# Two rings of weight buffers at fixed remainders, and another order of summing a pair's chunks

## The chip, the cores and the metric

The kernel runs on one core of one Trainium2 chip. The metric is the device time of the whole kernel in microseconds (us), as the median of several runs. Names used below: PE is TensorE, DVE is VectorE, ACT is ScalarE, SP the engine that issues the DMAs of the weights.

## The reference

Two layers work on x of 256 tokens by 1024 channels, all in float32. Each layer is a mixer and a ConvFFN, each followed by a layer norm. Cut to what matters here:

```python
def mixer_sublayer(x, ...):
    proj = x @ w_in        # RG-LRU input and GeLU gate, q/kv latents, rotary key, gates A and B
    y_rnn = jax.nn.gelu(g_rnn) * rg_lru(causal_dwconv(x_rnn, conv_w, conv_b), gx_w, gx_b, ...)
    y_mla = mla_attention(q_lat, kv_lat, k_rope, cos, sin, ...)
    merged = jax.nn.sigmoid(gate_a) * y_rnn + jax.nn.sigmoid(gate_b) * y_mla
    return merged @ w_out

def conv_ffn(x, w_up, ffn_conv_w, ffn_conv_b, w_down):
    h = causal_dwconv(x @ w_up, ffn_conv_w, ffn_conv_b)     # 1024 -> 6144
    h_gate, h_val = jnp.split(h, 2, axis=-1)
    return (jax.nn.gelu(h_gate) * h_val) @ w_down           # 3072 -> 1024

x = layer_norm(ALPHA * x + mixer_sublayer(x, ...), ...)
x = layer_norm(ALPHA * x + conv_ffn(x, ...), ...)
```

## The kernel before

Every float32 number is held as a sum of two numbers of the type fp32r, hi and lo, and a product is made of three matmuls: hi by hi, hi by lo and lo by hi (`mm3`, L193 to L196). Activations are kept as xhi and xlo, which begin at multiples of 256 bytes.

Weights come as raw tiles of 128 by 2048 numbers. SP loads one by `load_raw` (L156) into one of four raw buffers. `load_split` then splits it, half block by half block (1024 columns): ACT copies the raw half to hi (L185), DVE subtracts hi from raw to get lo (L186). A half block's hi and lo lie side by side in one tile `w` (L180), in a ring of six buffers. Each buffer is 8320 bytes long, so that the six begin, in the built program, at the remainders 192, 64, 192, 64, 192, 64 modulo 256. A half block takes the next buffer of the ring. Most raw tiles have two halves; a few have one, and after these the next raw tile's first half lies in the other sort of buffer. In layer 0's FFN, of 18 pairs that directly follow a down projection, six have their blocks at (192, 64), five at (64, 64) and seven at (192, 192); in layer 1's, twelve lie at (192, 64) and six at (64, 192).

A pair (`proj_pair`, L516 to L531) is one raw tile's product: 256 output channels, in two halves m of 128, by 1024 input channels in eight chunks kc. The first half block holds chunks 0 to 3, the second 4 to 7, each for both halves m. The loop at L525 runs over kc in order, so the 48 matmuls of a group (each of 256 columns) take 12 from the first block, 12 from the second, and the same again for the other m. The mixer's input projections call it (`g`, `x`, `ga`, `gb` in the ORDER table) and so does the up projection of the FFN, `up(j)` (L888); there a group is followed by 12 matmuls of 512 columns of the down projection (`dacc`). The weights of the down projection are split in the same way into other tiles (`wsh`, `wsl`). Other users of the `w` ring are the latent, q, k, v and output weights.

The order of PE is the written one. ACT, DVE and SP follow an order that a scheduler sets when the program is built, from its own estimates; a tile's reuse, and so the remainders, are set there too. Each engine works off its list in order and waits where an operand or a buffer isn't ready. In the mixer's recurrence, the convolved input is split into xch by ACT (L610) and xcl by DVE (L611), the block-diagonal gates multiply them on PE (`gates`), and L629 and L631 make the sigmoid gate sg and its product gl.

Of the kernel before, what the change touches and what calls it, by code (L numbers as in the profile page):

```python
# [11 lines left out]
F32 = mybir.dt.float32  # L12
F32R = mybir.dt.float32r
# [4 lines left out]
P = 128  # L18
# [3 lines left out]
KC = D // P  # L22
# [27 lines left out]
HELD = 4  # L50
WARM = 8
LINE = 256
STEP = 32
KORD = (0, 1, 4, 5, 2, 3, 6, 7)
NPAIR = DFF // P
ALPHA = (2 * DEPTH) ** 0.25
# [69 lines left out]
def trunk(ctx, tc, x_tok, x_chan, pos, wts, par, lnrow, consts, out):  # L126
# [8 lines left out]
    wpool = ctx.enter_context(tc.tile_pool(name="wpool", bufs=1))  # L135
# [4 lines left out]
    def slot(name, dt=F32):  # L140
        return big.tile([P, 1024], dt, tag="t4", name=name, bufs=19, align_bytes=LINE)

    def bank(name):
        return pp.tile([P, 512], F32, tag="pb", name=name)
# [4 lines left out]
    def load_raw(l, key, parts=None, between=None):  # L149
        o, n = WOFF[key]  # L150
        raw = wpool.tile([P, 2048], F32, tag="raw", name=f"raw{l}", bufs=4, align_bytes=LINE)
        src = wts[l, o:o + P * n].rearrange("(p n) -> p n", p=P)
        for i, (a, b) in enumerate(parts or ((0, n),)):
            if between and b == n:
                between()
            nc.sync.dma_start(out=raw[:, a:b], in_=src[:, a:b])  # L156
        return raw
# [3 lines left out]
    def behind(ins, first):  # L161
        if first is not None:
            tc.add_manual_dep(ins.ins, first.ins.name, no_sync, reason="issue order")

    last_split = [None]
    ready = [(None, None)]
    later = [False]

    def load_split(l, key, cuts, in_slots=False, after=(None, None),
                   step=1024, parts=None, between=None):  # L170
        raw = load_raw(l, key, parts, between)
        if later[0]:
            after = ready[0]
        n = WOFF[key][1]
        res = []
        for a, b in cuts:
            if in_slots:
                hi, lo = slot("wsh", F32R), slot("wsl", F32R)
            else:
                both = wpool.tile([P, 2048 + STEP], F32R, tag="w", name="w", bufs=6)  # L180
                hi, lo = both[:, :1024], both[:, 1024:2048]
            for c in range(a, b, step):
                d = min(c + step, b)
                h, w = hi[:, c - a:d - a], raw[:, c:d]
                behind(A.activation(h, w, AF.Copy), after[0])  # L185
                lo_ins = V.tensor_tensor(out=lo[:, c - a:d - a], in0=w, in1=h.bitcast(F32),  # L186
                                         op=ALU.subtract)
                behind(lo_ins, after[1])
                last_split[0] = lo_ins
            res.append((hi, lo))  # L190
        return res

    def mm3(o, lh, ll, rh, rl, start, stop):  # L193
        T.matmul(o, lhsT=lh, rhs=rh, start=start, stop=False)  # L194
        T.matmul(o, lhsT=lh, rhs=rl, start=False, stop=False)  # L195
        T.matmul(o, lhsT=ll, rhs=rh, start=False, stop=stop)  # L196
# [19 lines left out]
    def latent_weights(l, i, **kw):  # L216
        r = load_split(l, ("lat", i), ((0, LATW), (LATW, 2 * LATW)), l > 0 and i == 3, **kw)
        return [(2 * i + j, r[j]) for j in range(2)]
# [128 lines left out]
    def xsl(xs, kc, a=0, b=S):  # L347
        hi, lo = xs[kc // 4]
        o = (kc % 4) * S
        return hi[:, o + a:o + b], lo[:, o + a:o + b]  # L350
# [160 lines left out]
    for l in range(DEPTH):  # L511
# [3 lines left out]
        def fetch(key):  # L515
            held[key] = load_split(l, key, ((0, 1024), (1024, 2048)), after=ends)  # L516

        def proj_pair(key, r=None):
            if r is None:
                if key not in held:  # L520
                    fetch(key)
                r = held.pop(key)
            ps = bank("proj")
            for m in range(2):
                for kc in range(KC):  # L525
                    hi, lo = r[kc // 4]
                    o = (kc % 4) * 256 + m * P
                    rh, rl = xsl(xs, kc)
                    mm3(ps[:, m * S:(m + 1) * S], hi[:, o:o + P], lo[:, o:o + P],
                        rh, rl, kc == 0, kc == KC - 1)  # L530
            return ps  # L531

        gl = [slot("gl") for _ in range(2)]
# [1 line left out]
        def gelu_branch(i):  # L535
            ps = proj_pair(("g", i))
            act_step(A.activation(gl[i // 2][:, (i % 2) * 512:(i % 2) * 512 + 512], ps,
                                  AF.Gelu_apprx_tanh))
# [56 lines left out]
        def conv_branch(i):  # L595
            ps = proj_pair(("x", i))
            for m in range(2):
                c = 2 * i + m
                dst = xc[c // 4][:, (c % 4) * S:(c % 4) * S + S]
                src = ps[:, m * S:(m + 1) * S]  # L600
                A.activation(dst, src, AF.Identity, scale=pcol(l, "cw", 24 + c),
                             bias=pcol(l, "cb", c))
                for k in range(1, 4):
                    conv_end.append(V.scalar_tensor_tensor(
                        out=dst[:, k:], in0=src[:, :S - k], scalar=pcol(l, "cw", 8 * (3 - k) + c),
                        in1=dst[:, k:], op0=ALU.mult, op1=ALU.add,
                    ))
                xh = sm.tile([P, S], F32R, tag="k1", name="xch", bufs=13, align_bytes=LINE)
                xl = sm.tile([P, S], F32R, tag="k1", name="xcl", bufs=13, align_bytes=LINE)
                A.activation(xh, dst, AF.Copy)  # L610
                V.tensor_tensor(out=xl, in0=dst, in1=xh.bitcast(F32), op=ALU.subtract)  # L611
                xsp[c] = (xh, xl)
# [13 lines left out]
        def gate_branch(i):  # L626
            ps = proj_pair(("ga", i))
            sg = slot("sg")[:, :512]
            act_step(A.activation(sg, ps, AF.Sigmoid))  # L629
            dst = gl[i // 2][:, (i % 2) * 512:(i % 2) * 512 + 512]  # L630
            V.tensor_tensor(out=dst, in0=dst, in1=sg, op=ALU.mult)  # L631
# [52 lines left out]
        def group_begin(g):  # L684
            r = load_split(l, ("qk", g), ((0, GRP_A), (GRP_A, GRP_N)),
                           after=(None, turned[0]))
            q96 = slot("q96")[:QK].rearrange("p (h s) -> p h s", h=4)
            k96 = slot("k96")[:QK].rearrange("p (h s) -> p h s", h=4)
            nc.sync.dma_start(out=k96[NOPE:], in_=krot[:, None, :].to_broadcast([ROPE, 4, S]))
            qk[g] = (r, q96, k96)  # L690
# [373 lines left out]
```

## Time and profile before

| | |
|---|---|
| runs | 785.43, 785.65, 787.75 us; median 785.65 |
| profiled execution | 786.62 us, its span 784.8 us |
| PE busy | 770.5 us (98%) |
| DVE busy | 646.0 us (82%) |
| ACT busy | 510.2 us (65%) |
| chain that ended last | PE 89%, DVE 4%, ACT 4% |
| proj matmuls | 3648 of 256 columns, 278 ns each as recorded |

A matmul's record is longer than the distance from one start to the next, since matmuls are pipelined: the pace is read from the starts in the timeline. "Idle" before an instruction stands in brackets with the engine and operation that ended it. PEclk is the granted clock of PE, 1.00 being 2.4 GHz and 0.50 being 1.2 GHz.

### The profile page before, as it was taken

How to read it: one execution, taken by the hardware profiler on the slowest of the kernel's cores; microseconds unless marked ns; L12 is line 12 of the kernel's file. 1: busy time of each engine (PE TensorE's matmuls, PEld its weight loads, DVE VectorE, ACT ScalarE, POOL GpSimd, SP SyncE). 2: the span in 40 equal slices, each digit the busy share in tenths (PEclk: the TensorE clock that was granted, in tenths of full speed). 3: DMA queues.
4: the chain of work that ended last, by engine and by line, in shares of the span. 5: the costliest groups of instructions: out<-in, count | busy, mean ns of one | idle time of the engine just before them, and what ended most of it. 6: DMA issues, size and time to landing. Idle time of an engine off the chain costs nothing.

```text
span 784.8 us, 14452 instructions
## 1 busy us (share of the span) xinstructions
PE 770.5 (98%) x5712; PEld 723.9 (92%) x5712; DVE 646.0 (82%) x1260; ACT 510.2 (65%) x910; POOL 10.2 (1%) x27
## 2 busy tenths in 40 slices
PE   9999899999999999999999999999999999999996
PEld 9999899878999999999899999998799999999994
DVE  6998789997699977668777897999877998677665
ACT  6856887783677565556374579688657775565540
POOL 0000000000000000000000000000000000000000
PEclk9999999999999999999999999999999999999999
DMA  9855436525457555535715554463515675746311
GB/s 320 331 210 215 151 112 240 207 63 210 162 199 262 203 199 210 195 126 196 268 52 218 169 208 134 172 231 123 193 76 186 261 251 182 247 162 200 123 54 54
DMA packets 26467, 144.76 MB, mean 184 GB/s; under 512 B 3360, under 2 KB 7072, under 8 KB 11808
## 3 DMA queue, kind: packets, MB, share of 16 engines
q1 hardware_dynamic: 26400, 143.84, 51.7%
q8 instruction: 45, 0.74, 0.4%
q14 instruction: 22, 0.18, 0.1%
HBM read 140.68 MB, written 1.05 MB: 181 GB/s over the span
## 4 chain that ended last, share of the span: by engine, by line
PE 89%; DVE 4%; ACT 4%; issue 2%; DMA 1%; SPq 0%; DVEq 0%
PE proj L196 16%; PE proj L194 15%; PE proj L195 15%; PE dacc L194 6%; PE dacc L195 6%; PE dacc L196 6%; PE oacc L194 2%; PE oacc L196 2%; PE oacc L195 2%; PE sps L759 2%; DVE w L186 2%; PE yps L802 2%; PE ptp L787 1%; PE latp L195 1%; PE latp L196 1%
## 5 line engine op out<-in xcount | busy, mean ns | idle before, releaser
L196 PE MATMUL proj<-xhi,w 128*128 128x256 f32 x1216 | 338.0, 278 | 3.0 <-DVE w L186 3.0
L194 PE MATMUL proj<-xhi,w 128*128 128x256 f32 x1216 | 338.1, 278 | 0.0
L195 PE MATMUL proj<-xlo,w 128*128 128x256 f32 x1216 | 337.7, 278 | 0.0
L186 DVE TENSOR_TENSOR w<-raw,w 128x1024 fp32r<-128x1024 f32 (+5 forms) x226 | 241.8, 1087 | 52.4 <-ACT w L185 51.9
L185 ACT ACTIVATE w<-raw 128x1024 fp32r<-128x1024 f32 (+5 forms) x226 | 208.8, 952 | 86.6 <-PE proj L196 73.4
L196 PEld LDWEIGHTS proj<-xhi,w 128*128 128x128 f32 x1216 | 228.8, 188 | 3.4 <-DVE w L186 3.4
L195 PEld LDWEIGHTS proj<-xlo,w 128*128 128x128 f32 x1216 | 229.2, 189 | 1.3
L194 PEld LDWEIGHTS proj<-xhi,w 128*128 128x128 f32 x1216 | 228.9, 188 | 1.4
L905 DVE SCALAR_TENSOR_TENSOR u<-proj,par,u 128x255 f32<-128x255 f32 (+1 forms) x176 | 83.4, 478 | 25.4 <-ACT u L902 23.3
L902 ACT ACTIVATE u<-proj,par 128x256 f32<-128x256 f32 x88 | 49.7, 564 | 72.7 <-DVE u L905 47.8
L194 PE MATMUL dacc<-wsh,hh 128*128 128x512 f32 x192 | 75.2, 392 | 0.0
L195 PE MATMUL dacc<-wsl,hh 128*128 128x512 f32 x192 | 75.1, 391 | 0.0
L196 PE MATMUL dacc<-wsh,hl 128*128 128x512 f32 x192 | 74.7, 389 | 0.0
L186 DVE TENSOR_TENSOR wsl<-raw,wsh 128x1024 fp32r<-128x1024 f32 (+2 forms) x66 | 70.4, 1077 | 0.0
L185 ACT ACTIVATE wsh<-raw 128x1024 fp32r<-128x1024 f32 (+2 forms) x66 | 59.5, 938 | 0.0
L196 PEld LDWEIGHTS dacc<-wsh,hl 128*128 128x128 f32 x192 | 36.1, 188 | 7.8
L194 PEld LDWEIGHTS dacc<-wsh,hh 128*128 128x128 f32 x192 | 36.0, 188 | 6.4
L195 PEld LDWEIGHTS dacc<-wsl,hh 128*128 128x128 f32 x192 | 36.1, 188 | 6.0
L199 ACT ACTIVATE hh<-u 128x256 fp32r<-128x256 f32 x48 | 19.8, 411 | 24.7 <-DVE u L913 24.6
L194 PE MATMUL oacc<-w,mhi 128*128 128x512 f32 x64 | 26.7, 417 | 0.0
L196 PE MATMUL oacc<-w,mlo 128*128 128x512 f32 x64 | 25.3, 395 | 0.0
L195 PE MATMUL oacc<-w,mhi 128*128 128x512 f32 x64 | 25.2, 393 | 0.0
(213 smaller groups left out, 1130.2 us busy)
## 6 DMA issues: line engine op xcount, KB each, us to landing
raw<-in_wts SPq DMA_DIRECT2D x114, 1024.0 KB, 4.9
raw<-in_wts SPq DMA_DIRECT2D x8, 832.0 KB, 4.9
gb<-in_lnrow SPq DMA_DIRECT2D x8, 512.0 KB, 7.7
raw<-in_wts SPq DMA_DIRECT2D x4, 672.0 KB, 4.0
raw<-in_wts SPq DMA_DIRECT2D x7, 336.0 KB, 6.1
raw<-in_wts SPq DMA_DIRECT2D x4, 512.0 KB, 4.8
xres<-in_x_tok SPq DMA_DIRECT2D x2, 512.0 KB, 6.0
k<-krot SPq DMA_DIRECT2D x8, 128.0 KB, 2.4
```

The lines of the kernel that those rows point to most:

```text
L185: behind(A.activation(h, w, AF.Copy), after[0])
L186: lo_ins = V.tensor_tensor(out=lo[:, c - a:d - a], in0=w, in1=h.bitcast(F32), op=ALU.subtract)
L194: T.matmul(o, lhsT=lh, rhs=rh, start=start, stop=False)
L195: T.matmul(o, lhsT=lh, rhs=rl, start=False, stop=False)
L196: T.matmul(o, lhsT=ll, rhs=rh, start=False, stop=stop)
L199: A.activation(hi, src, AF.Copy)
L759: T.matmul(sps[:, P:P + S], lhsT=q96[:, h4, P:], rhs=k96[:, h4], start=True, stop=True)
L787: T.transpose(ptp[:, b * P:(b + 1) * P], sns[hh][:, b * P:(b + 1) * P], ident)
L802: T.matmul(yps[hh * 64:hh * 64 + 64, t * P:S], lhsT=vs[:, hv:hv + 64], rhs=pts[hh][:, 2 * t * P:(2 + t) * P], start=t == 0, stop=t == 1)
L902: ea = A.activation(dst, src, AF.Identity, scale=pcol(l, "fw", 96 + ch), bias=pcol(l, "fb", ch))
L905: ev = V.scalar_tensor_tensor(out=dst[:, k:], in0=src[:, :S - k], scalar=pcol(l, "fw", 48 * (2 - k) + ch), in1=dst[:, k:], op0=ALU.mult, o ...
```

## The change

The ring of six `w` buffers becomes two rings of three: `w0` for the first half block of a raw tile, `w1` for the second. The buffers are 8192 bytes long, and a tile of 128 bytes stands between the two rings. In the built program the `w0` buffers all begin at 192 modulo 256, the `w1` buffers all at 64; the activations still begin at multiples of 256. A pair sums its chunks in the order 0, 4, 5, 1, 2, 3, 6, 7, for both m.

```diff
@@ -50,7 +50,8 @@
 LINE = 256
-STEP = 32
+GAP = 32
+PORD = (0, 4, 5, 1, 2, 3, 6, 7)
 KORD = (0, 1, 4, 5, 2, 3, 6, 7)
@@ -162,6 +163,7 @@
+    gap = []
     last_split = [None]
@@ -173,11 +175,13 @@
-        for a, b in cuts:
+        for i, (a, b) in enumerate(cuts):
             if in_slots:
                 hi, lo = slot("wsh", F32R), slot("wsl", F32R)
             else:
-                both = wpool.tile([P, 2048 + STEP], F32R, tag="w", name="w", bufs=6)
+                if i and not gap:
+                    gap.append(wpool.tile([P, GAP], F32, name="gap"))
+                both = wpool.tile([P, 2048], F32R, tag=f"w{i % 2}", name=f"w{i % 2}", bufs=3)
                 hi, lo = both[:, :1024], both[:, 1024:2048]
@@ -522,12 +526,12 @@
             for m in range(2):
-                for kc in range(KC):
+                for kc in PORD:
                     hi, lo = r[kc // 4]
                     o = (kc % 4) * 256 + m * P
                     rh, rl = xsl(xs, kc)
                     mm3(ps[:, m * S:(m + 1) * S], hi[:, o:o + P], lo[:, o:o + P],
-                        rh, rl, kc == 0, kc == KC - 1)
+                        rh, rl, kc == PORD[0], kc == PORD[-1])
```

Lines behind the edit stand four later in the new kernel: L186 is L190 there, L525 is L529.

On PE, a group of layer 0's FFN begins so before; `w_3748` is its first half block, `w_3751` its second:

```order
L194 MATMUL proj_3754<-xhi_2359,w_3748 128x256
L195 MATMUL proj_3754<-xlo_2360,w_3748 128x256
L196 MATMUL proj_3754<-xhi_2359,w_3748 128x256
...
L194 MATMUL proj_3754<-xhi_2361,w_3751 128x256
L195 MATMUL proj_3754<-xlo_2362,w_3751 128x256
L196 MATMUL proj_3754<-xhi_2361,w_3751 128x256
```

and so in the new kernel, where `w0_3749` and `w1_3752` are the same two half blocks:

```order
L198 MATMUL proj_3755<-xhi_2360,w0_3749 128x256
L199 MATMUL proj_3755<-xlo_2361,w0_3749 128x256
L200 MATMUL proj_3755<-xhi_2360,w0_3749 128x256
L198 MATMUL proj_3755<-xhi_2362,w1_3752 128x256
L199 MATMUL proj_3755<-xlo_2363,w1_3752 128x256
L200 MATMUL proj_3755<-xhi_2362,w1_3752 128x256
```

The first three rows stand four times before the second block's first; now they stand once.

On ACT, at layer 1's gates, the order before is this; `raw1_5548` is the weight tile whose halves are `w_5550` and `w_5553`, `gates_5573` a gate bank:

```order
L622 ACTIVATE ga_4875<-gates_5573,par1_168 128x256
L185 ACTIVATE w_5550<-raw1_5548 128x1024
L610 ACTIVATE xch_5458<-xc_4872 128x256
L185 ACTIVATE w_5553<-raw1_5548 128x1024
L629 ACTIVATE sg_5631<-proj_5582 128x512
L622 ACTIVATE gx_4874<-gates_5634,par1_168 128x256
```

and this in the new kernel:

```order
L626 ACTIVATE ga_4876<-gates_5574,par1_169 128x256
L189 ACTIVATE w0_5551<-raw1_5549 128x1024
L189 ACTIVATE w1_5554<-raw1_5549 128x1024
L633 ACTIVATE sg_5632<-proj_5583 128x512
L614 ACTIVATE xch_5459<-xc_4873 128x256
L626 ACTIVATE gx_4875<-gates_5635,par1_169 128x256
```

The copy to xch has moved behind the second half block and sg; on DVE xcl has likewise moved behind both lo halves and the product gl.

On DVE, ahead of layer 1's last gate pair, the order before is this; `raw1_6009` is that pair's weight tile, `w_6011` its first half block and `w_6014` its second:

```order
L186 TENSOR_TENSOR w_5971<-raw1_5969,w_5971 128x768
L664 SCALAR_TENSOR_TENSOR th_5742<-ga_4876,gx_4874 128x1024
L186 TENSOR_TENSOR w_5974<-raw1_5969,w_5974 128x896
L186 TENSOR_TENSOR w_5982<-raw1_5980,w_5982 128x1024
L186 TENSOR_TENSOR w_6011<-raw1_6009,w_6011 128x1024
L186 TENSOR_TENSOR w_6014<-raw1_6009,w_6014 128x1024
```

and this in the new kernel:

```order
L190 TENSOR_TENSOR w0_5972<-raw1_5970,w0_5972 128x768
L668 SCALAR_TENSOR_TENSOR th_5743<-ga_4877,gx_4875 128x1024
L190 TENSOR_TENSOR w1_5975<-raw1_5970,w1_5975 128x896
L190 TENSOR_TENSOR w0_5983<-raw1_5981,w0_5983 128x1024
L190 TENSOR_TENSOR w1_6015<-raw1_6010,w1_6015 128x1024
L190 TENSOR_TENSOR w0_6012<-raw1_6010,w0_6012 128x1024
```

The two halves of that pair have changed places, the second block's being split first; layer 0's last gate pair has the same exchange.

## Rows read from the trace of the kernel before

**Rows 1.** The page, part 1: busy us of each engine (share), xinstructions
```profile
PE 770.5 (98%) x5712; PEld 723.9 (92%) x5712; DVE 646.0 (82%) x1260; ACT 510.2 (65%) x910; POOL 10.2 (1%) x27
```

**Rows 2.** Two FFN windows: us, busy PE PEld DVE ACT POOL, PEclk, DMA, GB/s
```profile
229.60:377.00 147.40, 147.40 (x1069) 139.11 (x1068) 119.26 (x185) 91.03 (x137) 0.00 (x0) 1.00 0.59 206
614.50:763.00 148.50, 148.50 (x1081) 139.71 (x1080) 116.87 (x181) 87.13 (x133) 0.00 (x0) 1.00 0.53 187
```

**Rows 3.** DVE and PE, layer 1's last gate pair: start us, us, instruction
```profile
498.66 5.34 DVE L186 TENSOR_TENSOR w<-raw,w 128x896 fp32r<-128x896 f32 x5
...
502.05 0.38 PE L196 MATMUL proj<-xhi,w 128*128 128x256 f32 x1 [1.51 <-DVE w L186]
```

**Rows 4.** Timeline of PE, ends of four groups (columns as in Rows 3)
```profile
55.10 0.28 PE L194 MATMUL proj<-xhi,w 128*128 128x256 f32 x1
...
60.54 0.28 PE L194 MATMUL proj<-xhi,w 128*128 128x256 f32 x1
...
246.36 0.28 PE L194 MATMUL proj<-xhi,w 128*128 128x256 f32 x1
...
252.01 0.40 PE L194 MATMUL dacc<-wsh,hh 128*128 128x512 f32 x1
...
254.74 0.28 PE L194 MATMUL proj<-xhi,w 128*128 128x256 f32 x1
...
256.51 0.28 PE L194 MATMUL proj<-xhi,w 128*128 128x256 f32 x1
...
260.25 0.40 PE L194 MATMUL dacc<-wsh,hh 128*128 128x512 f32 x1
...
622.84 0.28 PE L194 MATMUL proj<-xhi,w 128*128 128x256 f32 x1
...
628.38 0.40 PE L194 MATMUL dacc<-wsh,hh 128*128 128x512 f32 x1
```

**Rows 5.** DVE and PE, one split of layer 0's FFN and its group
```profile
287.09 1.22 DVE L186 TENSOR_TENSOR w<-raw,w 128x1024 fp32r<-128x1024 f32 x1
...
304.81 0.28 PE L194 MATMUL proj<-xhi,w 128*128 128x256 f32 x1
```

**Rows 6.** Timeline of ScalarE (ACT), VectorE and PE at layer 1's gates
```profile
468.05 1.06 ACT L185 ACTIVATE w<-raw 128x1024 fp32r<-128x1024 f32 x1 [2.09 <-PE proj L196]
469.01 0.40 ACT L610 ACTIVATE xch<-xc 128x256 fp32r<-128x256 f32 x1
...
469.15 1.23 DVE L186 TENSOR_TENSOR w<-raw,w 128x1024 fp32r<-128x1024 f32 x1 [0.67 <-ACT w L185]
470.29 0.42 DVE L611 TENSOR_TENSOR xcl<-xc,xch 128x256 fp32r<-128x256 f32 x1
470.62 1.22 DVE L186 TENSOR_TENSOR w<-raw,w 128x1024 fp32r<-128x1024 f32 x1
471.76 0.68 DVE L631 TENSOR_TENSOR gl<-gl,sg 128x512 f32<-128x512 f32 x1
472.36 0.61 DVE L640 TENSOR_SCALAR ga<-ga,kl 128x256 f32<-128x256 f32 x2
...
471.36 0.28 PE L195 MATMUL gates<-xcl,w 128*128 128x256 f32 x1
```

**Rows 7.** Timeline of VectorE and PE, first pair of layer 0, then its gates
```profile
20.79 1.22 DVE L186 TENSOR_TENSOR w<-raw,w 128x1024 fp32r<-128x1024 f32 x1
...
21.63 0.28 PE L196 MATMUL proj<-xhi,w 128*128 128x256 f32 x1
...
84.59 0.58 PE L195 MATMUL gates<-xcl,w 128*128 128x256 f32 x1 [1.44 <-DVE xcl L611]
```

**Rows 8.** Windows, around waits of layer 0 (columns as in Rows 2)
```profile
80.94:84.53 3.59, 1.52 (x9) 0.92 (x7) 3.59 (x8) 3.59 (x8) 0.00 (x0) 1.00 0.83 281
84.53:87.94 3.41, 3.35 (x15) 3.35 (x16) 3.16 (x7) 3.41 (x7) 0.00 (x0) 0.50 0.38 104
115.10:118.50 3.40, 1.89 (x16) 1.69 (x16) 3.40 (x4) 0.73 (x2) 0.00 (x0) 1.00 0.86 289
```

## The prediction

> **What bounds the kernel now.** I read first the busy times of the page [rows 1], then the two long stretches of the ConvFFN by windows [rows 2], then TensorE's instructions one by one. TensorE is busy for 770.5 of 784.8 us; in the two FFN windows it is busy for the whole of 147.40 and 148.50 us, while VectorE has 119.26 and 116.87 and ScalarE 91.03 and 87.13. In these stretches only TensorE's own pace counts, and a nanosecond a matmul is felt in full. In the two mixers it waits now and then for a half block that ScalarE and VectorE have yet to split; 1.51 us for a VectorE split is the kind [rows 3].
>
> That pace differs between groups of the same 48 matmuls [rows 4], the reader's first thing to see. A group is a pair's 48 matmuls of 256 columns; its length is the start of what follows less its own start. One inside the mixer takes 60.54 − 55.10 = 5.44, or 113.3 ns a matmul. In the FFN the one at 246.36 takes 5.65 (117.7 ns), the one at 254.74 5.51, the one at 622.84 5.54. What differs is where the two weight buffers lie. With (192, 192) all 48 run at 117.7, and so do the five (64, 64) groups. With (192, 64) the first 15, up to 256.51, take 1.77 or 118 ns each, and the other 33 take 3.74 or 113.3: the pace turns three matmuls after the step from the 192 block to the 64 block, and it stays fast when the group goes back to 192 for the second half. With (64, 192) the step from 192 to 64 comes only after 24 matmuls, and the gain is smaller. Of 30 such steps in slow stretches I found 29 with this turn; a step from 64 to 192 never made it. A mixer group that directly follows a fast one is fast throughout, whatever its blocks. Why the memory does this no row says; I use it as a pattern.
>
> **The change, part by part.** No matmul, copy or load is added; there are as many on each engine as before.
>
> *Pace.* Every pair now is (192, 64), and the step from 192 to 64 comes after 3 matmuls, so a group that starts slow should have some 6 slow matmuls and 42 fast ones: 5.44 + 6 × 0.0045 = 5.47. Layer 0's FFN: seven (192, 192) and five (64, 64) groups, 12 × 0.18 = 2.1; six (192, 64), 6 × 0.04 = 0.2. Layer 1's: twelve (192, 64), 0.5, and six (64, 192), 6 × 0.075 = 0.45. Outside the FFN, the slow (64, 64) group at layer 1's start is as long as the one at 246.36 and saves 0.18, the three behind it, the last pair of layer 0's mixer and the first FFN pair of either layer about 0.85 together (from nothing for a group fast already to 0.2). In all 4.3, between 1.2 (the pace turns only at the second step from 192 to 64, after 18 matmuls) and 5.6 (all of them wholly fast). In the FFN nothing is late next: a lo half that VectorE splits at 287.09 is first used by the group at 304.81 [rows 5], so that needing the second block 1.0 us earlier and letting the first go 0.7 us later stay covered. SP's loads wait for raw buffers, which those splits free, with the same cover.
>
> *Waits.* The second block is wanted after 3 matmuls, not 12: 9 × 0.1133 = 1.0 us earlier. The first is let go at position 6 of 8 of the second half, not at 4: 6 × 0.1133 = 0.7 us later. ScalarE takes its work in a fixed order, and each wait on a buffer holds what stands behind it.
> (a) The last pair of a mixer's gate branch waits 1.51 for its first block, in a run of five VectorE splits of 5.34 [rows 3]. The order now has the second block of that pair split ahead of the first, so the lo half that TensorE wants comes one split later: 5.34/5 = 1.07, and 1.14 for a full half; +1.1 in each layer. In layer 0 this wait is set by VectorE's queue, so that lesser delays of TensorE ahead of it (below) are swallowed by it.
> (b) Layer 1's gates. ScalarE now copies w0, w1 and does sg before xch. From [rows 6]: w0 starts at 468.05 + 0.68 (its buffer is free later); two copies at 0.96 (469.01 less 468.05) and sg at about 0.5 put xch near 471.2, ahead of VectorE's turn. VectorE then has w0, w1 and the gated product ahead of xcl: 469.15 + 0.68 + 1.14 + 1.14 (471.76 less 470.62) + 0.60 (472.36 less 471.76) = 472.7, and 0.42 for xcl itself makes 473.1. TensorE wants xcl at 471.36 and waits for nothing now. It will wait 1.75. Behind it the next pairs queue, and ScalarE and VectorE wait for those, so most of the loss goes on; I add 0.2 for a second block that then comes just late.
> (c) The first pair: the lo half of its second block starts at 20.79 on VectorE and is done by 22.0; the sixth matmul, now the first to want it, stands at 21.63 [rows 7]. +0.4. (d) Layer 0's gates: xcl stands behind two splits and more; today TensorE waits 1.44 there. From nothing (rope work is put earlier) to 2.4 (two splits at 1.2); I take 0.2. (c) and (d) go into the wait (a).
> Sum: 1.1 + 1.75 + 0.2 + 1.1 = 4.15, say 4.3 with what of (c) and (d) isn't swallowed; from 2.3 (two times 1.1) to 6.7.
>
> *Clock.* After a stretch of 3.59 us with 1.52 busy the granted clock stood at 0.50, the 1.2 GHz level, for 3.41 us, with 16 weight loads, 213 ns a matmul in place of 113: 16 × 0.1 = 1.6. After the 1.51 wait (1.89 busy of 3.40) it stayed at 1.00 [rows 8]. With 1.1 more of waiting the same 3.40 has about 0.8 busy, nearer to the first. There are two such places and a new wait at the gates. Below nothing, above three times 1.6 = 4.8; I take one, 1.6, since the stretch that fell had several waits in a row.
>
> Sum: −4.3 + 4.3 + 1.6 = +1.6. The profiled execution took 786.62, 0.97 above the median 785.65 of its runs; on it 788.2, on the median 787.2.
>
> **The rivals.** *No half-speed stretch*: the same sum without the 1.6, 785.6. For it: the two waits of 1.51 caused none. *Two*: 788.8; for it: both long waits are alike, so one seldom falls alone.
> *The pace turns late* (the slower side). Its place is every group of the FFN: three matmuls on the 192 block may be too few to bring the turn, which no row shows with fewer than 12; then the second step, after 18 matmuls, brings it, and a group takes 5.44 + 21 × 0.0045 = 5.54. The 12 slow groups gain 0.11 each, 1.3; the 18 of (192, 64) lose 0.03 each, 0.5; the six (64, 192) stand still; some 0.4 elsewhere: 1.2 in place of 4.3, and 785.65 − 1.2 + 4.3 + 1.6 = 790.3. It decides from a group length of about 5.51 on, today's. Against it: the turn comes with the first 64 block each time, three matmuls in.
> *The waits of layer 1 are paid once* (faster). If VectorE loses little by TensorE's 1.75 at the gates, then the wait of (a) shrinks by it, as in layer 0, and layer 1 costs 1.2 in place of 3.0: 785.65 − 4.3 + 2.4 = 783.7 without a half-speed stretch, and 783.0 with groups that are fast from their first matmul on (30 × 0.025). For it: VectorE's splits run back to back there; against: ScalarE's work in between waits for TensorE's groups.
> *Placement decides nothing*: what differs is which block follows which operation, the buffers' remainders merely go with it, and the gain is 0: 785.65 + 4.3 + 1.6 = 791.5. The Trainium skill, "SBUF — State Buffer", section "SBUF: two separate sides", speaks for this one: TensorE, ScalarE and VectorE's dedicated pair never wait on one another. By that rule 5.65 and 5.51 for the same group should not differ; the trace has them [rows 4], so the rule, as far as I can apply it, disagrees with the measurement here.
>
> **How the numbers follow.** This kernel's runs can tell about 0.3%, 2.4 us, from no change: 783.3 to 788.0. Forecast 0.36 at 787.2; no half-speed stretch 0.16 at 785.6; two 0.16 at 788.8; late turn 0.10 at 790.3; waits paid once 0.18 at 783.0 to 783.7; placement nothing 0.04 at 791.5. Faster: 0.15 of the 0.18. Slower: 0.16 + 0.10 + 0.04, and 0.06 of the forecast's own spread, 0.36. Same: the rest, 0.49. The range 783.0 to 790.0 leaves out the last case, half of the late turn and a third of the fastest, some 0.15.
>
> **What would show it.** FFN groups of 5.47, all alike (5.54 says late turn; 5.65 or a mixture, nothing); xcl released near 473 with a wait of 1.75 at layer 1's gates; waits of some 2.6 to 2.8 before both last gate pairs, with a split of the second block just ahead of the first; the clock row of the 3.4 us behind them at 0.50 or 1.00; the FFN windows together 3.2 shorter. The forecast fails if the groups' pace isn't set by the step, or if VectorE's order alone doesn't set these waits.

## The result, and the profile after

The changed kernel takes 790.54 us (median of 11 runs, 787.96 to 793.43), the kernel before in the same comparison 786.83 (11 runs, 785.11 to 787.75). The ratio is 1.0052, with a 95% interval of 1.0034 to 1.0069: slower by half a per cent. The forecast was 787.2 with a range of 783.0 to 790.0; the time lies outside it, and a rise of 1.6 that was forecast came out as 3.7.

The profiled execution has a span of 788.1 against 784.8. The page of the profile after, busy time by engine:

```profile
PE 768.5 (98%) x5712; PEld 720.6 (91%) x5712; DVE 647.2 (82%) x1260; ACT 504.6 (64%) x910; POOL 10.9 (1%) x27
```

TensorE works 2.0 us less [rows 1] and the span is 3.3 us longer: it waits more. First the two FFN stretches, by windows over the same work as [rows 2] (us, busy by engine, granted clock, DMA share, GB/s):

```profile
233.10:378.40 145.30, 145.30 (x1069) 136.81 (x1068) 118.04 (x183) 87.71 (x136) 0.00 (x0) 1.00 0.58 210
618.80:766.30 147.50, 147.50 (x1080) 138.72 (x1080) 117.10 (x181) 85.46 (x133) 0.00 (x0) 1.00 0.53 188
```

They are 2.1 and 1.0 us shorter. Next, in the timeline of PE after, the group that answers to the one at 246.36 [rows 4], and the five long waits (start, us, instruction, idle before it and its releaser):

```profile
23.53 0.38 PE L200 MATMUL proj<-xhi,w 128*128 128x256 f32 x1 [0.59 <-DVE w L190]
...
86.75 0.38 PE L199 MATMUL gates<-xcl,w 128*128 128x256 f32 x1 [2.24 <-DVE xcl L615]
...
118.98 0.38 PE L200 MATMUL proj<-xhi,w 128*128 128x256 f32 x1 [2.67 <-DVE w L190]
...
249.61 0.28 PE L198 MATMUL proj<-xhi,w 128*128 128x256 f32 x1
...
250.32 0.28 PE L198 MATMUL proj<-xhi,w 128*128 128x256 f32 x1
...
255.08 0.40 PE L198 MATMUL dacc<-wsh,hh 128*128 128x512 f32 x1
...
473.95 0.39 PE L199 MATMUL gates<-xcl,w 128*128 128x256 f32 x1 [1.21 <-DVE xcl L615]
...
506.19 0.39 PE L200 MATMUL proj<-xhi,w 128*128 128x256 f32 x1 [2.62 <-DVE w L190]
```

The group takes 255.08 − 249.61 = 5.47 in place of 5.65: six matmuls up to 250.32 at 118 ns, then 42 at 113.3. All 36 FFN groups behind a down projection but one are so (the one at 372.81 also waits, and takes 5.76). Of the waits, the one at 473.95 did not exist before [rows 6], and the two of 2.6 to 2.7 were 1.51 (layer 1's in [rows 3]). What a wait costs is read from the starts around it, since the idle time in the brackets leaves out part: layer 1's last gates take from 469.98 to 474.65, 4.67 us, where they took from 469.21 to 471.93, 2.72. At layer 1's gates the timeline of DVE and ACT after shows the queue as the order said:

```profile
470.59 2.36 DVE L190 TENSOR_TENSOR w<-raw,w 128x1024 fp32r<-128x1024 f32 x2 [0.54 <-ACT w L189]
472.87 0.69 DVE L635 TENSOR_TENSOR gl<-gl,sg 128x512 f32<-128x512 f32 x1
473.47 0.42 DVE L615 TENSOR_TENSOR xcl<-xc,xch 128x256 fp32r<-128x256 f32 x1
```
```profile
469.50 2.01 ACT L189 ACTIVATE w<-raw 128x1024 fp32r<-128x1024 f32 x2 [2.09 <-PE proj L200]
471.42 0.57 ACT L633 ACTIVATE sg<-proj 128x512 f32<-128x512 f32 x1
471.89 0.40 ACT L614 ACTIVATE xch<-xc 128x256 fp32r<-128x256 f32 x1
```

xch is ready by 472.3, but xcl starts only at 473.47, behind two lo halves and gl.

The lengths of all groups of matmuls, before and after, add up to this (us, after less before, from the starts in both timelines):

| place | forecast | measured |
|---|---|---|
| pace, FFN and mixers | −4.3 | −4.2 |
| layer 0: first pair | +0.4 | +1.0 |
| layer 0: gates to the last gate pair | +0.9 (0.2 and 1.1, less 0.4 swallowed) | +1.5 |
| layer 0's FFN, last pair (wait) | 0 | +0.3 |
| layer 1: gates | +1.75 | +1.95 |
| layer 1: a second block just late | +0.2 | +0.3 |
| layer 1: last gate pair | +1.1 | +1.2 |
| landing of the very first weights | 0 | +0.9 |
| half-speed stretches in these two profiles | +1.6 | 0 (one each) |

Some 0.3 more is spread over attention. The waits are 6.3, not 4.3. The landing of the first weights is not counted as the change's: the first pair began anywhere between 20.7 and 22.0 in the kernels of the experiments, whatever their order. The first pair's own 1.0 is no firm figure either: with the same order and rings it took 6.54 here, and 6.77, 5.68 and 6.38 in e6, e9 and e10, against 5.50 before.

The granted clock, by windows of the kernel after:

```profile
116.00:119.40 3.40, 0.73 (x6) 0.54 (x6) 3.40 (x4) 1.08 (x2) 0.00 (x0) 1.00 0.80 279
119.40:122.82 3.42, 3.42 (x18) 3.42 (x17) 3.39 (x8) 0.00 (x0) 0.00 (x0) 0.50 0.95 388
503.30:506.70 3.40, 0.78 (x7) 0.58 (x6) 3.40 (x4) 1.03 (x2) 0.00 (x0) 1.00 0.90 301
506.70:510.12 3.42, 3.42 (x32) 3.42 (x32) 3.39 (x8) 0.00 (x0) 0.00 (x0) 1.00 0.96 379
```

Of two waits of one size, that at 118.98 was followed by 3.42 us at 0.50 and that at 506.19 by none. So it goes from run to run: the mean clock of the 11 runs was 0.996 in five (787.96 to 789.84 us), 0.994 in two (790.54 and 791.03), 0.991 in three (792.08 to 792.89) and 0.988 in one (793.43). A half-speed stretch lowers the mean by 3.42 × 0.5/788 = 0.0022; from 0.996 to 0.991 and to 0.988 are then 2.3 and 3.6 stretches, and by the medians of these runs (788.55, 792.53 and 793.43) one costs some 1.3 to 1.8 us. The median run has 0.994, one stretch more than the profiled one. The 57 runs of the kernel before in the experiments' comparisons stood, but for two, at 0.995 to 0.998.

### The profile page after: what moved, and what is told of

Read it like the earlier page. It is cut to its first block, busy times and chain, and to the rows that moved or that the text cites. A ratio compares the mean times of both kernels' runs of the same rounds, so it can differ in the third digit from the quotient of the medians.

```text
span 788.1 us, 14456 instructions
## 1 busy us (share of the span) xinstructions
PE 768.5 (98%) x5712; PEld 720.6 (91%) x5712; DVE 647.2 (82%) x1260; ACT 504.6 (64%) x910; POOL 10.9 (1%) x27
## 4 chain that ended last, share of the span: by engine, by line
PE 86%; DVE 5%; ACT 5%; issue 2%; DMA 1%; SPq 0%; POOL 0%; DVEq 0%; ACTq 0%
PE proj L200 15%; PE proj L199 15%; PE proj L198 15%; PE dacc L198 6%; PE dacc L199 6%; PE dacc L200 6%; DVE w L190 2%; PE oacc L198 2%; PE oacc L200 2%; PE oacc L199 2%; PE sps L763 2%; PE yps L806 2%; PE ptp L791 1%; ACT w L189 1%; PE sps L761 1%
## 5 line engine op out<-in xcount | busy, mean ns | idle before, releaser
L190 DVE TENSOR_TENSOR w<-raw,w 128x1024 fp32r<-128x1024 f32 (+5 forms) x226 | 241.3, 1088 | 49.0 <-ACT w L189 48.4
L190 DVE TENSOR_TENSOR wsl<-raw,wsh 128x1024 fp32r<-128x1024 f32 (+2 forms) x66 | 69.4, 1078 | 0.0
```

## Experiments

Two theories are tested. The first (all runs but e7 and e8): the loss is in the mixers, from two sources that add, the rings (which exchange the splits of the last gate pairs) and the chunk order (which delays xch and xcl at the gates), and delays of TensorE are passed on, not swallowed. Rivals: one of the two parts makes all of it; or the clock does. The second (e7 and e8): the step from a 192 block to a 64 block makes the pace. Each ratio is to the kernel before in the same comparison: its median was 787.22 beside e1 to e4 (29 runs), 786.67 beside e5 to e8 (13) and 786.22 beside e9 to e11 (15).

**The rings alone (e1).**

```diff
-                for kc in PORD:
+                for kc in range(KC):
-                        rh, rl, kc == PORD[0], kc == PORD[-1])
+                        rh, rl, kc == 0, kc == KC - 1)
```

> The two rings alone, chunks in their natural order 0 to 7. Theory (two sources of waits that add): every pair is now (192, 64), so a slow-start FFN group takes 5.51: 12 x 0.14 in layer 0 and 6 x 0.035 in layer 1, and some 0.5 in the mixers, -2.4 in all; the split order at the two last gate pairs is exchanged, so the waits there grow from 1.5 to about 2.6, +2.3; layer 1's gates wait for nothing. Net about 0, 785.5 to 788.5 with up to one more half-speed stretch. Rival (all the loss comes with the rings): 790. Rival (all the loss comes with the chunk order): 784.4, the waits staying at 1.5.

790.0 (12 runs, ratio 1.0032, 1.0017 to 1.0047). FFN groups of 5.51 and layer 1's gates without a wait, as expected; the last gate pairs in PE's timeline:

```profile
118.61 0.38 PE L200 MATMUL proj<-xhi,w 128*128 128x256 f32 x1 [2.65 <-DVE w L190]
...
504.18 0.38 PE L200 MATMUL proj<-xhi,w 128*128 128x256 f32 x1 [2.66 <-DVE w L190]
```

So the longer waits there come with the rings. The time is 1.5 above the expected range: its profile has three half-speed stretches, one behind each of these waits and one at layer 0's gates. It is also the very figure of the rival "all the loss comes with the rings", and the time alone would have spoken for it; the profile does not, since the wait at layer 1's gates is missing here and the FFN's groups are slower than in the whole change.

**The chunk order alone (e2)**, in the old ring of six, as an edit of the kernel before:

```diff
+PORD = (0, 4, 5, 1, 2, 3, 6, 7)
-                for kc in range(KC):
+                for kc in PORD:
-                        rh, rl, kc == 0, kc == KC - 1)
+                        rh, rl, kc == PORD[0], kc == PORD[-1])
```

> The chunk order alone, in the old ring of six. Theory: the (192, 64) groups take 5.47, the (64, 64) and (192, 192) ones stay at 5.65, the (64, 192) ones step from 192 to 64 after 9 matmuls and take about 5.50: -1.1 in all; layer 1's gates wait 1.5 to 2, the first pair 0.8, layer 0's gates about 0.5 more than before, two small ones 0.3 each; the last gate pairs still wait 1.5 and no more. Net +2.5 to +3, about 789.5. Rival (the rings bring the waits): gates without wait, 785.7. Rival (a step from 192 to 64 needs more than three matmuls on 192): no group of 5.47.

797.33 (6 runs, ratio 1.0124, 1.0101 to 1.0146), 8 us above what I expected. The pace came out as said (5.47, 5.65, 5.48 for the three sorts), and so did the wait at layer 1's gates, the first row. The last gate pairs wait 1.5 and 1.3 for their first half and, against what I expected, 0.5 more for their second. The largest part of the rest is at a place that I had not looked at: the output product and attention, whose splits of output weights also moved; the stretch from the last gate pair to the FFN is 1.9 us longer in each layer.

```profile
478.56 0.39 PE L196 MATMUL gates<-xcl,w 128*128 128x256 f32 x1 [1.21 <-DVE xcl L612]
...
166.47 0.51 PE L195 MATMUL oacc<-w,mhi 128*128 128x512 f32 x1 [0.49 <-DVE k L733]
...
175.18 1.24 PE L803 MATMUL yps<-pT,v 128*64 128x256 f32 x8 [0.68 <-ACT pT L791]
```

The wait at 166.47 ends with VectorE's copy of k, attention's keys, which here stands behind two splits of output weights. Before, it stood ahead of them (e2's rows, then the kernel before's):

```profile
165.01 0.68 DVE L187 TENSOR_TENSOR w<-raw,w 128x512 fp32r<-128x512 f32 x1
165.73 0.69 DVE L733 COPY k<-kps 64x512 f32<-64x512 f32 x1
```
```profile
160.34 0.69 DVE L732 COPY k<-kps 64x512 f32<-64x512 f32 x1
...
161.35 0.68 DVE L186 TENSOR_TENSOR w<-raw,w 128x512 fp32r<-128x512 f32 x1
```

The whole change doesn't have this wait: there the copy, at 164.10, is again ahead of the splits, at 165.10. So the two parts' costs do not simply add, and "the rings bring all" and "the order brings all" both fall.

**The rings, and the new order only in the FFN's first halves (e3).**

```diff
+            first = PORD if r is not None else range(KC)
-                for kc in PORD:
+                for k, kc in enumerate(range(KC) if m else first):
-                        rh, rl, kc == PORD[0], kc == PORD[-1])
+                        rh, rl, k == 0, k == KC - 1)
```

> The two rings, and the new chunk order only in the FFN's up projections and there only in the first half m = 0 (natural order in m = 1 and in the mixers). Theory: FFN groups of 5.47 as with the whole change (-3.2), the mixers' slow groups -0.5, no wait at layer 1's gates nor a longer one at the first pair; the two exchanged splits +2.3. Net -1.4, about 785.4, or 787 with a half-speed stretch after the long waits. Rival (the clock alone makes the loss): as many half-speed stretches as with the whole change, 789.

787.04 (12 runs, ratio 0.9996, 0.9981 to 1.0011): the FFN's gain is whole (5.47), no wait at layer 1's gates, 2.65 at the last pairs. It fits the theory with one half-speed stretch more (its profile has two, the kernel before's one). The FFN groups are as long as in the whole change, which has the new order in m = 1 too; so what the whole change loses beyond this run, it loses in the mixers.

**The same, with the halves in order for all tiles (e4).** Here `prev` is the pair of the first half's instructions.

```diff
+                if not in_slots and i:
+                    behind(hi_ins, prev[0])
+                    behind(lo_ins, prev[1])
```

> As the run before, and each raw tile's second half block is issued for splitting behind its first half block on both engines, as it stood before at the last gate pairs. Theory: the waits there go back to 1.5, nothing else is late: net -3.7, about 783, and no more half-speed stretches than before. Rival (the exchanged splits are harmless, the waits come from three buffers in place of six): the waits stay at 2.7 and the time at 785.4 or above.

A miss: 788.1 (12 runs, ratio 1.0005, 0.9992 to 1.0018). The waits before the last gate pairs went back to 1.5, but the rule also put two splits of output weights ahead of the copy of k (158.70 and 160.10, then 161.16), and TensorE now waits in the output product, as in e2:

```profile
161.90 0.51 PE L204 MATMUL oacc<-w,mhi 128*128 128x512 f32 x1 [1.01 <-DVE k L743]
...
170.60 1.24 PE L813 MATMUL yps<-pT,v 128*64 128x256 f32 x8 [0.66 <-ACT pT L801]
```

**The rule for the last gate pair alone (e5).**

```diff
-                if not in_slots and i:
+                if i and key == ("gb", 3):
```

> The two rings, the new chunk order only in the FFN's up projections in the half m = 0, and the two halves split first-then-second only for the last gate pair of each layer (so that the output weights' splits keep the order that the rings give). Theory: waits of 1.5 before the last gate pairs as in the kernel before, no wait in the output product, FFN groups of 5.47: -3.2 there, -0.6 in the mixers, 783.0 to 783.8 against 787; a ratio of 0.995. Rival (the mixer's other groups lose what the FFN gains, as with the first-then-second rule for all tiles): 787.

783.08 (5 runs, ratio 0.9958, 0.9945 to 0.9971), as expected; the last gate pair of layer 1 waits as before:

```profile
499.86 0.38 PE L206 MATMUL proj<-xhi,w 128*128 128x256 f32 x1 [1.52 <-DVE w L192]
```

**The whole change with both orders put back (e6).** `xc_last` holds the instructions of the convolved input's last xch and xcl.

```diff
+        prev = xc_last[0] if key == ("gb", 0) else (None, None)
+                if key == ("gb", 0) or i and key == ("gb", 3):
+                    behind(hi_ins, prev[0])
+                    behind(lo_ins, prev[1])
```

> The whole change, with two places of the order put back by hand: the last gate pair's first half is split before its second, and the convolved input's xch and xcl stand ahead of the two halves of the weight tile behind them. Theory (the loss is these two): layer 1's gates wait for nothing (-1.9), the last gate pairs wait 1.5 (-1.1 each), and with them goes one half-speed stretch (-1.6): 784.5 to 786 against 790.5 for the whole change. Rival (the pair's earlier need of its second block is what costs, order or not): 788 to 790, with new waits at the pairs behind.

784.26 (8 runs, ratio 0.9969, 0.9958 to 0.9980), 6.3 less than the whole change and 0.2 below the expected range. In its PE timeline neither gate stretch has a wait over 0.5, and the last gate pair now waits twice:

```profile
500.07 0.39 PE L207 MATMUL proj<-xhi,w 128*128 128x256 f32 x1 [1.48 <-DVE w L193]
...
501.20 0.38 PE L207 MATMUL proj<-xhi,w 128*128 128x256 f32 x1 [0.51 <-DVE w L193]
```

**Each order by itself, on the whole change (e9, e10).** First the gates':

```diff
-                if key == ("gb", 0) or i and key == ("gb", 3):
+                if key == ("gb", 0):
```

> The whole change with one place put back by hand: the convolved input's xch and xcl stand ahead of the halves of the weight tile behind them (both layers); the last gate pairs keep the second half first. Theory (each delay of TensorE in the mixer is passed on by VectorE, so waits add and don't swallow one another): layer 1's gates -1.9, layer 0's gates -2.3 (a wait of 2.4 there becomes none), the waits of 2.8 before the last gate pairs stay: 786 to 787 against 790.5. Rival (what is saved ahead is waited for at the last gate pairs, VectorE's queue setting them): waits there of 4 to 5, 789 to 790.

785.02 (11 runs, ratio 0.9986, 0.9977 to 0.9995), more than 5 below the whole change and 1 below the expected. This is the run that decides on swallowing. Layer 0's gates fall from 5.91 (81.53 to 87.44) to 3.65 and TensorE comes to the last pair at 112.18, 3.75 earlier than at 115.93. Of that 2.26 are the gates, 0.86 the first pair and 0.67 the landing of the first weights. Its wait there is as long as ever, since VectorE's run of splits is earlier by nearly the same (110.67 against 114.46). PE of the whole change, PE here, then DVE here:

```profile
81.53 0.28 PE L198 MATMUL gates<-xch,w 128*128 128x256 f32 x1
...
87.44 0.28 PE L198 MATMUL proj<-xhi,w 128*128 128x256 f32 x1
...
115.93 0.28 PE L198 MATMUL proj<-xhi,w 128*128 128x256 f32 x1
```
```profile
79.99 0.28 PE L205 MATMUL gates<-xch,w 128*128 128x256 f32 x1
...
83.64 0.28 PE L205 MATMUL proj<-xhi,w 128*128 128x256 f32 x1
...
112.18 0.28 PE L205 MATMUL proj<-xhi,w 128*128 128x256 f32 x1
...
115.19 0.39 PE L207 MATMUL proj<-xhi,w 128*128 128x256 f32 x1 [2.62 <-DVE w L193]
```
```profile
110.67 2.20 DVE L193 TENSOR_TENSOR w<-raw,w 128x896 fp32r<-128x896 f32 x2
```

Not all of the 5.5 undoes a loss of the change: in the kernel before layer 0's gates waited 1.44 for xcl too, with a half-speed stretch behind [rows 7] [rows 8], and this edit removes that as well.

Then the last gate pair's:

```diff
-                if key == ("gb", 0):
+                if i and key == ("gb", 3):
```

> The whole change with only the last gate pair's first half split ahead of its second. Theory: the first half's wait goes back to 1.65, and the second half, wanted after 3 matmuls, then waits 0.7: -0.4 in each layer, and if it is the single long wait that brings the half-speed stretch behind it, one stretch less: 788 to 789.7. Rival (the exchange alone accounts for the 1.1 of each wait): -2.3 and a stretch less, 786.6.

789.33 (5 runs, ratio 1.0036, 1.0024 to 1.0049): −1.2, inside the expected range. At the last pairs the order gives back only 0.4 in layer 0 and 0.3 in layer 1 (8.11 in place of 8.41), because the chunk order asks for the second half at once; that the rest of the 1.2 is a half-speed stretch less is not shown, the median clock being 0.994 in both kernels. Layer 1's last pair in PE's timeline:

```profile
505.41 0.39 PE L206 MATMUL proj<-xhi,w 128*128 128x256 f32 x1 [1.53 <-DVE w L192]
...
506.54 0.38 PE L206 MATMUL proj<-xhi,w 128*128 128x256 f32 x1 [0.52 <-DVE w L192]
```

**What makes the pace (e7, e8).** The kernel of e5 with both rings at 192:

```diff
-GAP = 32
+GAP = 64
```

> As e5, but both rings at 192 modulo 256 and nothing else changed. Theory (a step from a 192 block to a 64 block turns the pace): no step, all 36 FFN groups behind a down projection take 5.65 in place of 5.47, +6.5, about 790. Rival (the order of the chunks makes the pace, not the remainders): 5.47, 783.5.

791.91 (4 runs, ratio 1.0069, 1.0056 to 1.0082), 8.8 above e5. In the traces PE, ACT and DVE do the same instructions in the same order as in e5; what differs is where the second ring begins, and a group takes 253.40 − 247.75 = 5.65. The time is 1.9 above the 790 expected: layer 0's mixer, fast in e5, runs at the slow pace here too. With a gap ahead of the first ring as well, the rings lie at 64 and 192; one run:

```diff
-                if i and not gap:
-                    gap.append(wpool.tile([P, GAP], F32, name="gap"))
+                if len(gap) <= i:
+                    gap.append(wpool.tile([P, GAP], F32, name=f"gap{i}"))
```

> As e5, but the first ring at 64 and the second at 192 modulo 256. Theory: the step from 64 to 192 after 3 matmuls does nothing, that from 192 to 64 after 9 turns the pace: 12 slow matmuls, groups of 5.50. Rival (any step turns it): 5.47. Rival (the first ring's remainder counts): 5.44 or 5.65.

782.01, and 258.51 − 253.03 = 5.48, with 9 matmuls at 118 ns. In the order of the chunks the step from 64 to 192 comes after 3 matmuls and the one back to 64 after 9; the pace turns with the second and not with the first. PE's timelines of the two:

```profile
247.75 0.28 PE L204 MATMUL proj<-xhi,w 128*128 128x256 f32 x1
...
253.40 0.40 PE L204 MATMUL dacc<-wsh,hh 128*128 128x512 f32 x1
```
```profile
253.03 0.28 PE L204 MATMUL proj<-xhi,w 128*128 128x256 f32 x1
...
258.51 0.40 PE L204 MATMUL dacc<-wsh,hh 128*128 128x512 f32 x1
```

The Trainium skill, "SBUF — State Buffer", section "SBUF: two separate sides", has TensorE wait on no other engine at its ports. Read as a promise that a buffer's place costs nothing, which the section does not say in so many words, it does not hold here, by 5.65 against 5.47. What TensorE loses these 4 ns a matmul to, no run shows.

**The best of them (e11)**: the kernel of e5 with the two edits of e6:

```diff
-                if i and key == ("gb", 3):
+                if key == ("gb", 0) or i and key == ("gb", 3):
```

> The rings, the new chunk order only in the FFN's first halves, the last gate pair's halves in the old order (as e5), and xch and xcl ahead of the weight tile behind them. Theory: layer 0's gates lose the wait of 1.4 that the kernel before has too and the half-speed stretch behind it: 783.1 - 1.7 - 1.0 = 780.4, a ratio of 0.992. Rival (the last gate pair waits for what was saved): 782 to 783.

780.99 (5 runs, 780.51 to 781.34, ratio 0.9929, 0.9916 to 0.9941), faster than both kernels. Its waits, by what PE waits for (us in total, times, longest):

```profile
PE proj L207 <- DVE w L193: 3.0, 2, 1.5
PE gates L206 <- DVE xcl L623: 1.3, 2, 0.8
```

No half-speed stretch falls in its profile before the last 5 us, and its five runs are within 0.83 us.

## Why the prediction was wrong

*The pace was right.* −4.3 was forecast, −4.2 measured, the FFN windows 3.1 shorter (3.2 forecast), the group 5.47 to the digit. The late turn and "placement decides nothing" fall with it, and e7 shows the last directly. By the time alone the late turn would have passed: its 790.3 is 0.2 from the measured 790.54, and only the groups' length, 5.47 and not 5.54, tells that this is chance.

*Layer 1's gates and last gate pairs were right in place and nearly in size*: 1.95 for 1.75, 1.2 for 1.1. For the last pairs e10 corrects the reason: the exchange of the splits costs 1.1 only while the first block is what is wanted; with the new chunk order all but 0.3 of layer 1's 1.2 (0.4 in layer 0) is lost without the exchange too.

*The step that failed in its mechanism* is "(c) and (d) go into the wait (a)", with "lesser delays of TensorE ahead of it are swallowed by it". I took VectorE's queue before the last gate pair for a clock of its own. It isn't. In the timelines of DVE before and then after, the recurrence waits for ScalarE by the same 1.91, and all of it stands 0.90 later:

```profile
105.43 2.36 DVE L662 TENSOR_TENSOR gx<-gx,th 128x1024 f32<-128x1024 f32 x2 [1.91 <-ACT th L654]
...
113.56 5.34 DVE L186 TENSOR_TENSOR w<-raw,w 128x896 fp32r<-128x896 f32 x5
```
```profile
106.33 2.36 DVE L666 TENSOR_TENSOR gx<-gx,th 128x1024 f32<-128x1024 f32 x2 [1.91 <-ACT th L658]
...
114.46 5.47 DVE L190 TENSOR_TENSOR w<-raw,w 128x896 fp32r<-128x896 f32 x5
```

TensorE comes to that pair at 115.93 in place of 115.05, 0.88 later. Both engines move together, and the wait stays whole. By itself this pair of rows does not decide it, since the first weights, which landed 0.9 later, move both engines too; e9 does, where 3.1 us saved at the first pair and the gates reach VectorE's splits in full and the wait stays 2.62. My reading of the row showed who releases the wait, not what that engine had waited for 8 us earlier; the gates' results feed the recurrence, and the recurrence stands ahead of the splits. The rival "waits of layer 1 are paid once" rested on the same error, and I gave it 0.18. Had I let the delays add, layer 0 would have cost 1.1 + 0.4 + 0.2 and both layers 4.75.

*Most of what the waits cost beyond the forecast is size, not swallowing.* The swallowing hid 0.45, which would have put the forecast at 787.7. The other 1.5 of the measured 6.3 are: the first pair 0.6 more than I took (the runs scatter there by more than that); two second blocks of layer 0 that come 0.25 and 0.3 late and that I had at nothing, the second of them in the FFN's last pair, where I wrote that nothing is late next; and 0.4 more in layer 1.

*The clock*: one half-speed stretch more was taken, and the median run has about that; the profiled run has none more. Which wait brings it is not settled: two waits alike differ in one profile, and in e9 a stretch falls behind layer 1's pair and not behind layer 0's.

*The base.* 1.2 of the 3.3 between 787.2 and 790.54 is the median of before, 785.65 in the three runs shown and 786.83 in eleven; the other 2.1 are the waits. On the later median the same sum gives 788.4, and the time would have stood inside a range of the same width.

## What to carry to other kernels

A wait for an engine with a queue is followed back until it meets work that doesn't depend on the waiting engine; only then can it swallow a delay. Where a scheduler sets the order, a change of a buffer or of an inner loop is priced with the new order on every engine and in every stage, and what pays in one stage (here the FFN's first halves) is made there alone. Remainders of buffer addresses were worth 4% of a matmul here (117.7 against 113.3 ns), which a timeline shows as two paces of the same instruction.

## What the runs showed that I had not expected

With both rings at 192, the pace is 117.7 ns nearly everywhere, and yet layer 1's mixer runs at 113.3 from the group behind the latents' transposes on (430.16 to 435.60 is 5.44). So a step from a 192 block to a 64 block is one way to turn the pace and not the only one; what else does is open. In the order of 64 and 192 the turn came at once, after 9 slow matmuls, where I had expected 12.
